# Layer 1's heads: the wait for recurrent states, eight places for them, and three row blocks of the first head loaded early

## The chip, the cores and the metric

The kernel runs on one core of one Trainium2 chip. The metric is the device time of one execution in microseconds; lower is better. The profile is that of one execution of the same program. Engine names are those of the profile: PE is the matrix engine (PEld its weight loads), ACT the scalar engine, DVE the vector engine, POOL the GpSimd engine, SP the engine that only issues transfers.

## The reference, cut to what matters

The program is a two-layer streaming encoder step for 512 prompt tokens and 8 running sequences of 16 tokens each (640 tokens, width 2048). Layer 0 is stick-breaking attention; layer 1, which this change is in, is gated linear attention (GLA) with 4 heads, 256 key and 512 value channels each:

```
q_in = q * exp(b)                                     # b: running sum of the log decays
a = einsum('bchd,bshd->bhcs', q_in, k * exp(-b)), kept for s <= c
o = einsum('bhcs,bshe->bche', a, v) + einsum('bchd,bhde->bche', q_in, S)
S = exp(b_last)[..., None] * S + einsum('bshd,bshe->bhde', k * exp(b_last - b), v)
o = o * rsqrt(mean(o * o) + EPS) * g_out
y = (o * silu(r)) @ w_out
```

The prompt starts from a zero state S and goes through it in blocks. Each of the 8 running sequences brings a state of its own (256 x 512 floats a head) that is read from HBM, used, updated and written back. After the heads, y = (4 heads x 512 channels) @ w_out, with the 2048 rows of w_out handled as 16 row blocks of 128 (kt 0 to 15; head h owns kt 4h to 4h+3).

## The kernel before, in words

Every product of two full-precision numbers is done as three products of rounded parts (hi x hi, hi x lo, lo x hi). `halves` makes the parts: ACT casts the high one (L134), DVE subtracts to get the low one (L135).

The order of PE's instructions is the order in which the Python program emits them. The other engines' queues are ordered by the compiler's own timeline, so a load on SP or a cast on ACT can run well ahead of the place where it stands in the text, as soon as its data and its place in memory allow. The program keeps a clock of its own, `pe["now"]`, which adds an estimate for each matmul. Around a main stream of matmuls it runs side lanes: Python generators that `yield step(wait, tp, z, tiled)` and are resumed by `Side.tick`, which the main stream calls every few matmuls, once `wait` on that clock has passed. In `tick`, lanes that are due and not marked `tiled` run first; then follows

```
            tiled = [x for x in due if x in self.lanes and x[1][2]]
            if tiled and pe["now"] >= self.tiled_at + self.every:
```

The list `due` was made at the start of the tick. A lane that has just run in this tick, and now stands at a `tiled` step, is in that list still; it is run a second time at once, and the wait of its new step is not looked at.

The stage of this change is "layer 1's heads". Its main stream is, in this order:

- `others` (L653, in `plain`): the q and k products of heads 1 to 3, 12 of them in 24 items of 48 matmuls of 320 columns. It ends with head 3's k. The h2 operand lies in the 32 large places t0 to t31; the 12 places t20 to t31 are free once the last item but one has ended.
- `share(0)`, then `share(1)` (L699): the output product's rows of head 0 (kt 0 to 3) and of head 1 (kt 4 to 7), 240 matmuls of 512 columns each. `share(g)` may begin when `came["rows"] >= 4 * g + 4` row blocks are split into the places, and 2.0 us of the program's clock after the last of them; until then `side.until` lets only the side lanes run and moves the clock on by 0.2.
- the tail (L368, L2004): rows of heads 2 and 3, residual, norm and stores.

The side lanes are:

- `decays`: decay factors of a head (L1638 on PE, tables of exp and log on ACT), then q and k scaled by them. Head 3's waits for the end of `others`.
- `prompt_lane`: 4 blocks of 128 tokens a head; scores L1566, products L1554, state S; it ends each block with `leave`, which transposes (L1601), multiplies by the gate (DVE L1602) and stores to `og_d[h]` (POOL L78, shown as og<-gate).
- `sample_lane`: the running sequences of a head, in 4 groups of 4 states: read each state with q (L1864, 8 matmul records a group), then update each (PE L1870, DVE L1872), store it, and ask for a new one in its place. There are `S0 = 7` places; an `ask` (POOL, shown as s<-in_state_gla) comes 7.0 us of the program's clock after the store (out_dram<-s) of the state that had the place. Before reading a group the lane does

```
                    while any(x not in states for x in group):
                        yield step(0.3)
                    yield step(max(since, max(states[x][1] for x in group) + 13.0) - pe["now"], tiled=True)
```

where `states[x][1]` is the clock at the ask. The step ahead of this one is never `tiled`.

- `fetches`: reads finished rows of `og_d` back (SP L71, shown as og_in<-og) into the two places of the tag "pl", which hold the outputs of `others` too, and splits them (`ogh`, `ogl`). All of kt 0 to 3 are asked for behind `came["last"]`, which is set in the middle of the last item of `others`, when the last output has its place.

The transfers of POOL (state loads and stores, gates, og<-gate) are issued in one queue, in order.

Of the kernel before, what the change touches and what calls it, by code (L numbers as in the profile page):

```python
# [8 lines left out]
F32 = mybir.dt.float32  # L9
# [6 lines left out]
P = 128  # L16
# [14 lines left out]
ZSCALE = 128 ** -0.5  # L31
TOK = T // P
WR = 2
S0 = 7
GP = 2
NPAIR = HEADS // 2
PLAIN = 2
# [4 lines left out]
def hybrid_step_kernel(ctx: ExitStack, tc: tile.TileContext, A: dict, O: list):  # L42
# [27 lines left out]
    def load(out, in_):  # L70
        nc.sync.dma_start(out=out, in_=in_)  # L71
# [61 lines left out]
    def halves(hi, lo, x, e=None):  # L133
        nc.scalar.copy(hi, x)  # L134
        (e or dve).tensor_tensor(lo, x, hi.bitcast(F32), op=ALU.subtract)  # L135
# [13 lines left out]
    def wraw(src, a, n):  # L149
        r = wp.tile([P, 1024], F32, tag="wr", name="wr", bufs=WR)[:, :a * n]  # L150
        load(r.rearrange("p (a n) -> p a n", a=a), src)
        return r
# [113 lines left out]
    def slot(n, shape=(P, T), dt=F32R, name="h"):  # L266
        return hp.tile(list(shape), dt, tag=f"t{n}", name=name)
# [6 lines left out]
    def step(wait=0.0, tp=0, z=0, tiled=False):  # L274
        return wait, tp, z, tiled

    class Side:
# [10 lines left out]
        def after(self, wait, what):  # L288

            self.due.append((pe["now"] + wait, what))  # L290
            self.due.sort(key=lambda x: x[0])

        def share(self, **bufs):
            self.free = {k: [0.0] * n for k, n in bufs.items()}
# [52 lines left out]
    def drive(*gens):  # L347
        for g in gens:
            for _ in g:
                side.tick()  # L350
# [331 lines left out]

    y_t = {}

    def share(g, og, w, leave=None, at=None, first=None):


        src = w.rearrange("(kt p) n -> p kt n", p=P)

        def raw(c, i):  # L690
            return wraw(src[:, 4 * g + 2 * i:4 * g + 2 * i + 2, 512 * c:512 * c + 512], 2, 512)

        def products(acc, a, i, w):
            wh, wl = w
            for e in range(2):
                kt = 4 * g + 2 * i + e
                h, lo = (x[:, P * a:P * a + P] for x in og[kt])
                for l, r, first, last in ((h, wh, True, False), (h, wl, False, False), (lo, wh, False, True)):
                    mm(acc, l, by(l, r[:, e, :]), start=i == 0 and e == 0 and first, stop=i == 1 and e == 1 and last)  # L699
                yield  # L700

        def add(a, c, pt):
            if g:
                dve.tensor_tensor(y_t[a, c], pt, y_t[a, c], op=ALU.add)  # L704
            else:
                y_t[a, c] = slot(5 * c + a, (P, 512), F32, "y")
                nc.scalar.copy(y_t[a, c], pt)

        leave = leave or add
        raws = list(first or [raw(0, 0), raw(0, 1)])  # L710

        def made():
            return [t.rearrange("p (a n) -> p a n", a=2) for t in split(raws.pop(0))]

        w0, w1 = made(), made()
        for c in range(4):
            ws = [w0, w1]
            if c < 3:
                raws += [raw(c + 1, 0), raw(c + 1, 1)]
            if at:  # L720
                at(c)
            each = (0, 1, 2) if leave is add or c < 3 else (4, 1, 2, 3, 0)
            for a in each:
                acc = bank("mm")
                for i in range(2):
                    yield from products(acc, a, i, ws[i])
                leave(a, c, acc)
                if a == each[0] and c < 3:
                    w0 = made()
            if len(each) == 3:  # L730
                acc = {a: bank("mm") for a in (3, 4)}
                for i in range(2):
                    for a in (3, 4):
                        yield from products(acc[a], a, i, ws[i])
                        if i:
                            leave(a, c, acc[a])
                    if i == 0 and c < 3:
                        w1 = made()
# [491 lines left out]
    with tc.tile_pool(name="o0", bufs=1, reuse_waits="tile") as po, ExitStack() as only_d:  # L1230
# [235 lines left out]
        n = 0  # L1466
# [32 lines left out]
    def w_of(g, c, i):  # L1499

        k0 = 4 * g + 2 * i
        return w_out1.rearrange("(kt p) n -> p kt n", p=P)[:, k0:k0 + 2, 512 * c:512 * c + 512]

    with tc.tile_pool(name="gl", bufs=1, reuse_waits="tile") as gl:
        came = {"plain": False, "last": False, "of": 0, "when": 0.0}

        def keep(dst, hh):
            t = []

            def leave(nt, pt):  # L1510
# [4 lines left out]
                if nt:  # L1515
                    nc.scalar.dma_start(out=dst[:, hh, :], in_=t[0])
                    for h in range(1, GH):
                        if hh and dst is gk_d[h]:
# [3 lines left out]

        others = plain(h2, src, [(n0 + P * hh, keep(dst, hh)) for h in range(1, GH)
                                 for n0, dst in ((256 * h, gq_d[h]), (NK + 256 * h, gk_d[h])) for hh in range(2)],
                       lambda: came.update(plain=True))
        for _ in range(2):
            next(others)

# [24 lines left out]
            for n, (a, b) in enumerate(((0, 0), (0, 1), (1, 0))):  # L1553
                mm(out, l[a], by(l[a], r[b]), start=start and n == 0, stop=stop and n == 2, skip_group_check=True)  # L1554

        masked = [gl.tile([P, P], F32, name=f"aT{n}") for n in range(3)]
        for t in masked:
            nc.gpsimd.memset(t, 0.0)
        turns = {"n": 0}
# [49 lines left out]
        def decays():  # L1609

            def weights(h):
                wa2 = gl.tile([96, 256], F32R, tag="wa2", name="wa2", bufs=2)
                load(wa2.bitcast(F32), wa2_d[:, 256 * h:256 * h + 256])
                yield step(4.0 if h else 8.0)
                return wa2
# [183 lines left out]
        def sample_lane():  # L1799
# [12 lines left out]
            for h in range(GH):  # L1812
# [43 lines left out]
                for n in range(4):  # L1856
                    dt, e = n // 2, n % 2
                    group = [(h, e, dt, m) for m in range(4)]
                    while any(x not in states for x in group):
                        yield step(0.3)  # L1860
                    yield step(max(since, max(states[x][1] for x in group) + 13.0) - pe["now"], tiled=True)
                    for m in range(4):
                        l = qz[e][:, dt, 32 * m:32 * m + 32]
                        mm(o[32 * m:32 * m + 32, :], l, by(l, states[group[m]][0]), start=False, stop=n == 3,  # L1864
                           skip_group_check=True)
                    for m in range(4):
                        yield step(0.3, tp=1)
                        pt = bank("tp")
                        l = kst[e][:, m, :]
                        mm(pt, l, by(l, vst[:, m, :]), start=True, stop=True)  # L1870
                        s0 = states[group[m]][0]
                        dve.scalar_tensor_tensor(s0, s0, es[:, dt, 2 * m + e:2 * m + e + 1], pt,  # L1872
                                                 op0=ALU.mult, op1=ALU.add)
                        side.after(1.0, lambda x=group[m]: leaves(x))
                    if n == 1:
                        yield from stack(1)
                        yield step(1.5)
# [5 lines left out]
                if h + 1 < GH:  # L1883
                    yield step(4.0)
                    here = fetch(h + 1)

        def fetches():

            def free(kt):
                g, s = kt // 4, kt % 4  # L1890
                return came["plain"] and came["shares"] >= min(2, g if s > 1 else g - 1)

            rows = {}

            def ask_rows(kt):
                rows[kt] = gl.tile([P, T], F32, tag="pl", name="og_in", bufs=2)
                load(rows[kt], og_d[kt // 4][:, kt % 4, :])

            for kt in range(10):
                while min(through.values()) <= kt // 4 or not came["last"]:  # L1900
                    yield step(0.5)
                if kt not in rows:
                    yield step(5.0)
                    ask_rows(kt)
                    if kt % 4 < 3 and kt < 9 and came["plain"]:
                        ask_rows(kt + 1)
                    yield step(4.0)
                while not free(kt):
                    yield step(0.3)
                n = 20 + 2 * kt % 12  # L1910
                og1[kt] = slot(n, name="ogh"), slot(n + 1, name="ogl")
                halves(*og1[kt], rows.pop(kt))
                if kt % 4 < 3 and kt < 9 and kt + 1 not in rows:
                    ask_rows(kt + 1)
                came["rows"], came["at"] = kt + 1, pe["now"]
                yield step(0.5)
# [2 lines left out]
        for x in (decays(), prompt_lane(), sample_lane(), fetches()):  # L1919
            side.add(x)  # L1920
        drive(others)
        with tc.tile_pool(name="w4", bufs=1, reuse_waits="tile") as w4:
            ring3["pool"] = w4
            first = [wraw(w_of(0, 0, i), 2, 512) for i in range(2)]
            for g in range(2):
                side.until(lambda: came["rows"] >= 4 * g + 4 and pe["now"] > came["at"] + 2.0)
                drive(share(g, og1, w_out1, first=first))
                came["shares"] = g + 1
                first = [wraw(w_of(g + 1, 0, i), 2, 512) for i in range(2)]
            ring3["pool"] = None  # L1930
            parts = [split(r) for r in first]
            first = [wraw(w_of(3, 0, i), 2, 512) for i in range(2)]
            side.finish()


    share_banks(mm=8)
# [96 lines left out]
```

## Time and profile before

| what | before |
|---|---|
| median of 3 runs | 2536.63 us (2534.40 to 2538.53) |
| the profiled execution's own time | 2535.51 us |
| its span from first to last instruction | 2533.8 us |
| PE busy | 2429.8 us (96% of the span) |
| DVE / ACT / POOL busy | 1581.8 / 995.2 / 163.6 us |
| layer 1's heads, `others` | about 1975 to 2243 us |
| `share(0)`, first to last matmul | 2266.8 to about 2353 us |
| `share(1)`, first to last matmul | about 2354 to 2411 us |

A row of the timeline has start and length in microseconds, engine, line, operation, tiles, count; in brackets stands how long the engine had been idle before it and what ended that. A row of the waits has who waited for whom: microseconds in total, times, longest. A row of a table by stretches has, for each engine, busy time and count, then the granted clock of PE (1.00 is full), the share of the DMA engines and GB/s.

### The profile page before, as it was taken

To read this page: it belongs to the slowest core of one execution; us is meant where nothing else is said; L and a number is where in the kernel's file an instruction comes from. 1 tells how busy PE (TensorE), PEld (TensorE's weight loads), DVE (VectorE), ACT (ScalarE), POOL (GpSimd) and SP (SyncE) were. 2 spreads that over 40 slices of the span, in tenths; PEclk is the share of its full clock that TensorE was granted. 3 is DMA by queue.
4 is the path that set the end of the run, shared out by engine and by line. 5 is a ranking of instruction groups with operands and counts; after the bars stand their busy time and mean duration, and the time that the engine had idled before them with its cause. 6 is when DMAs were issued, how large, how long until landed. Compare 5 with 4: busy or idle time off the path is not lost. (4 is left out here: it accounts for less than half of the span.)

```text
span 2533.8 us, 43960 instructions
## 1 busy us (share of the span) xinstructions
PE 2429.8 (96%) x17561; PEld 2150.1 (85%) x17561; DVE 1581.8 (62%) x2565; ACT 995.2 (39%) x1730; POOL 163.6 (6%) x390
## 2 busy tenths in 40 slices
PE   7899999999999989999999989999999999979998
PEld 5589999999999989888887768999999988857776
DVE  5575555555656655766775678666676565555556
ACT  4342222222223334555442345333333554545223
POOL 0010000000000000000000000000000233342100
PEclk8899999999999999999999999999999999989999
DMA  9966666766654357777864655354434778785634
GB/s 346 327 209 212 223 214 198 241 218 205 219 186 123 113 187 233 260 246 243 267 209 124 214 172 169 96 148 123 125 105 119 212 238 255 217 278 184 228 111 147
DMA packets 469439, 503.13 MB, mean 199 GB/s; under 512 B 42730, under 2 KB 366450, under 8 KB 469106
## 3 DMA queue, kind: packets, MB, share of 16 engines
q1 hardware_dynamic: 446274, 436.60, 54.8%
q0 software_dynamic: 16048, 51.92, 6.1%
q10 hardware_dynamic: 6912, 11.80, 1.3%
q8 instruction: 138, 2.26, 0.4%
q14 instruction: 67, 0.55, 0.1%
HBM read 411.10 MB, written 89.13 MB: 197 GB/s over the span
## 5 line engine op out<-in xcount | busy, mean ns | idle before, releaser
L594 PE MATMUL ps_mm<-sums,wh 128*128 128x320 f32 x2752 | 613.7, 311 | 1.5 <-ACT wh L134 1.5
L594 PE MATMUL ps_mm<-h,wh 128*128 128x320 f32 x2064 | 461.8, 312 | 5.7 <-DVE u L600 4.6
L594 PEld LDWEIGHTS ps_mm<-sums,wh 128*128 128x128 f32 x2752 | 458.3, 188 | 10.4 <-issue 7.4
L594 PE MATMUL ps_mm<-sums,wl 128*128 128x320 f32 x1376 | 425.8, 309 | 0.7 <-DVE wl L135 0.7
L135 DVE TENSOR_TENSOR wl<-wr,wh 128x1024 fp32r<-128x1024 f32 x193 | 236.1, 1224 | 244.0 <-ACT wh L134 243.2
L594 PEld LDWEIGHTS ps_mm<-h,wh 128*128 128x128 f32 x2064 | 343.2, 188 | 21.8 <-issue 13.0
L134 ACT CAST wh<-wb 128x1024 fp32r<-128x1024 f32 x170 | 178.4, 1049 | 426.1 <-PE ps_mm L594 352.8
L134 ACT CAST wh<-wr 128x1024 fp32r<-128x1024 f32 x193 | 202.6, 1050 | 346.6 <-PE ps_mm L594 184.6
L594 PE MATMUL ps_mm<-h,wl 128*128 128x320 f32 x1032 | 319.2, 309 | 0.0
L653 PE MATMUL ps_mm<-h,wh 128*128 128x320 f32 x1152 | 265.2, 318 | 5.3 <-ACT pl L1514 3.1
L594 PEld LDWEIGHTS ps_mm<-sums,wl 128*128 128x128 f32 x1376 | 258.4, 188 | 1.0 <-DVE wl L135 1.0
L135 DVE TENSOR_TENSOR wl<-wb,wh 128x1024 fp32r<-128x1024 f32 x170 | 207.9, 1223 | 60.5 <-ACT wh L134 60.1
L653 PEld LDWEIGHTS ps_mm<-h,wh 128*128 128x128 f32 x1152 | 193.0, 189 | 21.7 <-issue 11.4
L699 PE MATMUL ps_mm<-wh,ogh 128*128 128x512 f32 x450 | 197.4, 439 | 4.2 <-DVE y L704 2.7
L594 PEld LDWEIGHTS ps_mm<-h,wl 128*128 128x128 f32 x1032 | 193.8, 188 | 0.0
L653 PE MATMUL ps_mm<-h,wl 128*128 128x320 f32 x576 | 178.5, 310 | 0.0
L699 PE MATMUL ps_mm<-wh,ogl 128*128 128x512 f32 x450 | 177.9, 395 | 0.3 <-DVE ogl L135 0.3
L699 PE MATMUL ps_mm<-wl,ogh 128*128 128x512 f32 x450 | 177.7, 395 | 0.0
L699 PEld LDWEIGHTS ps_mm<-wh,ogh 128*128 128x128 f32 x450 | 85.6, 190 | 29.6 <-issue 14.4
L653 PEld LDWEIGHTS ps_mm<-h,wl 128*128 128x128 f32 x576 | 108.8, 189 | 0.0
L699 PEld LDWEIGHTS ps_mm<-wh,ogl 128*128 128x128 f32 x450 | 85.0, 189 | 20.3 <-DVE ogl L135 0.7
L518 PE MATMUL ps_mm<-wh,h 128*128 128x512 f32 x252 | 93.4, 432 | 5.9 <-ACT h L134 2.8
(355 smaller groups left out, 3747.0 us busy)
## 6 DMA issues: line engine op xcount, KB each, us to landing
ar<-in_w_ada_dram SPq DMA_DIRECT2D x160, 512.0 KB
wb<-in_sb_w_in_dram SPq DMA_DIRECT2D x82, 512.0 KB
kc<-in_cache_sb_k_dram SPq DMA_DIRECT2D x64, 512.0 KB
vc<-in_cache_sb_v_dram SPq DMA_DIRECT2D x64, 512.0 KB
wr<-in_gla_w_in_dram SPq DMA_DIRECT2D x51, 512.0 KB
wb<-in_gla_w_in_dram SPq DMA_DIRECT2D x45, 512.0 KB
wr<-in_sb_w_in_dram SPq DMA_DIRECT2D x44, 512.0 KB
ar<-in_w_ada_dram SPq DMA_DIRECT2D x64, 256.0 KB
```

Of the source, the lines that this page charges most:

```text
L134: nc.scalar.copy(hi, x)
L135: (e or dve).tensor_tensor(lo, x, hi.bitcast(F32), op=ALU.subtract)
L518: mm(acc[a], l, by(l, r[:, e, :]), start=j == 0 and e == 0 and begun, stop=j == 7 and e == 1 and last)
L594: mm(acc, l[:, k, :], by(l[:, k, :], r), start=start and k == 0 and first, stop=k == 7 and last, skip_group_check=True)
L653: mm(acc[nt], l[:, k, :], by(l[:, k, :], r), start=k0 == 8 and k == 0 and first, stop=k0 == 0 and k == 7 and last)
L699: mm(acc, l, by(l, r[:, e, :]), start=i == 0 and e == 0 and first, stop=i == 1 and e == 1 and last)
```

## The change: what it does

- The wait of a group of states is split into a step that is not `tiled`, `max(since, last ask + 9.0)`, and a `tiled` step of 0.0 behind it, so that the wait is kept.
- `S0` goes from 7 to 8. The memory for it comes from `wa2` (one place instead of two) and from two of the three `masked` tiles, which now lie in the shift and scale tables of layer 1's norm.
- The pool `w4` (a third pair of places for split weights, before opened behind `others`) is opened with the stage. When head 0 is done in both lanes, 8.0 later, kt 0, 1 and 2 of `og_d[0]` are loaded into its two tiles (four loads: kt 2 is cut in two pieces). They are split when the last item but one of `others` has ended. Only kt 3 still goes through "pl", without the extra wait of 5.0.
- `upper()`, called at the end of the last item but one, starts `share(0)`'s generator there: its first two weight loads and the first split are emitted at that place.

```diff
-S0 = 7
+S0 = 8
...
-        w0, w1 = made(), made()
+        w0 = made()
+        if apart:
+            yield
+        w1 = made()
...
-                       lambda: came.update(plain=True))
+                       lambda: upper())
...
-        masked = [gl.tile([P, P], F32, name=f"aT{n}") for n in range(3)]
+        masked = [t[1].rearrange("p k r -> p (k r)")[:, :P] for t in (sh_t, sc_t)] + [gl.tile([P, P], F32, name="aT2")]
...
-                wa2 = gl.tile([96, 256], F32R, tag="wa2", name="wa2", bufs=2)
+                wa2 = gl.tile([96, 256], F32R, tag="wa2", name="wa2")
...
-                    yield step(max(since, max(states[x][1] for x in group) + 13.0) - pe["now"], tiled=True)
+                    yield step(max(since, max(states[x][1] for x in group) + 9.0) - pe["now"])
+                    yield step(0.0, tiled=True)
...
+        begun = []
+
+        def upper():
+            came.update(plain=True)
+            begun.append(share(0, og1, w_out1, first=[wraw(w_of(0, 0, i), 2, 512) for i in range(2)], apart=True))
+            next(begun[0])
...
+            while min(through.values()) < 1:
+                yield step(0.5)
+            yield step(8.0)
+            x = [w4.tile([P, 1024], F32, tag=t, name="og_in") for t in ("wh", "wl")]
+            for n in range(2):
+                load(x[n][:, :T], og_d[0][:, n, :])
+            load(x[0][:, T:], og_d[0][:, 2, :1024 - T])
+            load(x[1][:, T:2 * T - 384], og_d[0][:, 2, 1024 - T:])
+            while not came["plain"]:
+                yield step(0.3)
+            for kt in range(2):
+                halves(*row(kt), x[kt][:, :T])
+                yield step(0.8)
+            to = row(2)
+            halves(*[t[:, :1024 - T] for t in to], x[0][:, T:])
+            halves(*[t[:, 1024 - T:] for t in to], x[1][:, T:2 * T - 384])
+            came["rows"], came["at"] = 3, pe["now"]
...
-            for kt in range(10):
+            for kt in range(3, 10):
                 while min(through.values()) <= kt // 4 or not came["last"]:
-                    yield step(0.5)
+                    yield step(0.3)
                 if kt not in rows:
-                    yield step(5.0)
+                    if kt > 3:
+                        yield step(5.0)
                     ask_rows(kt)
-                    if kt % 4 < 3 and kt < 9 and came["plain"]:
+                    if 3 < kt < 9 and kt % 4 < 3:
                         ask_rows(kt + 1)
                     yield step(4.0)
```

A second `self.due.sort` was added too; it sorts a list that is sorted already.

More of the change, by code (lines that the diff above doesn't have):

```diff
@@ L290, in after @@
             self.due.append((pe["now"] + wait, what))
+            self.due.sort(key=lambda x: x[0])
             self.due.sort(key=lambda x: x[0])
@@ L683, in hybrid_step_kernel, with share @@
     y_t = {}
-    def share(g, og, w, leave=None, at=None, first=None):
+    def share(g, og, w, leave=None, at=None, first=None, apart=False):
         src = w.rearrange("(kt p) n -> p kt n", p=P)
@@ L1502, in w_of @@
         return w_out1.rearrange("(kt p) n -> p kt n", p=P)[:, k0:k0 + 2, 512 * c:512 * c + 512]
-    with tc.tile_pool(name="gl", bufs=1, reuse_waits="tile") as gl:
+    with tc.tile_pool(name="gl", bufs=1, reuse_waits="tile") as gl, \
+            tc.tile_pool(name="w4", bufs=1, reuse_waits="tile") as w4:
         came = {"plain": False, "last": False, "of": 0, "when": 0.0}
@@ L1885, in sample_lane, with row @@
                     here = fetch(h + 1)
+        begun = []
[3 more added lines that the diff above has]
+            next(begun[0])
+        def row(kt):
+            n = 20 + 2 * kt % 12
+            og1[kt] = slot(n, name="ogh"), slot(n + 1, name="ogl")
+            return og1[kt]
         def fetches():
@@ L1890, in free @@
                 g, s = kt // 4, kt % 4
-                return came["plain"] and came["shares"] >= min(2, g if s > 1 else g - 1)
+                return came["shares"] >= min(2, g if s > 1 else g - 1)
+            while min(through.values()) < 1:
[15 more added lines that the diff above has]
+            came["rows"], came["at"] = 3, pe["now"]
             rows = {}
@@ L1909, in fetches @@
                     yield step(0.3)
-                n = 20 + 2 * kt % 12
-                og1[kt] = slot(n, name="ogh"), slot(n + 1, name="ogl")
-                halves(*og1[kt], rows.pop(kt))
+                halves(*row(kt), rows.pop(kt))
                 if kt % 4 < 3 and kt < 9 and kt + 1 not in rows:
@@ L1921, in hybrid_step_kernel @@
         drive(others)
-        with tc.tile_pool(name="w4", bufs=1, reuse_waits="tile") as w4:
+        for g in range(2):
+            side.until(lambda: came["rows"] >= 4 * g + 4 and pe["now"] > came["at"] + 2.0)
             ring3["pool"] = w4
[L1924 to L1933, printed above, removed]
+            drive(share(g, og1, w_out1, first=first) if g else begun[0])
+            came["shares"] = g + 1
+            first = [wraw(w_of(g + 1, 0, i), 2, 512) for i in range(2)]
+        ring3["pool"] = None
+        parts = [split(r) for r in first]
+        first = [wraw(w_of(3, 0, i), 2, 512) for i in range(2)]
+        side.finish()
     share_banks(mm=8)
```

## The prediction, as put on record before the changed kernel ran

> **What bounds the kernel.** I read first the page, then PE's waits over the stage, then PE's timeline at each long wait, then the queues that feed what PE waited for. First the page's busy times and PE's waits from 1966 to 2420 us:
>
> ```profile
> PE 2429.8 (96%) x17561; PEld 2150.1 (85%) x17561; DVE 1581.8 (62%) x2565; ACT 995.2 (39%) x1730; POOL 163.6 (6%) x390
> ...
> PE ps_z L1864 <- DMA s<-in_state_gla_dram: 23.4, 3, 17.4
> ...
> PE ps_mm L368 <- DVE y L704: 1.5, 1, 1.5
> PE ps_mm L699 <- DVE y L704: 1.1, 3, 0.5
> PE ps_mm L699 <- ACT y L707: 0.9, 1, 0.9
> ```
>
> PE is the bound, and nearly all that it loses in this stage is one wait: sample states that are not there when L1864 reads them. The three cases on PE's timeline, with the last matmul of `others` and the first of `share(0)`:
>
> ```profile
> 2081.52 1.04 PE L1864 MATMUL ps_z<-s,qz 128*32 128x512 f32 x2 [0.26 <-DMA s<-in_state_gla_dram]
> ...
> 2170.20 1.92 PE L1864 MATMUL ps_z<-s,qz 128*32 128x512 f32 x2 [5.69 <-DMA s<-in_state_gla_dram]
> ...
> 2242.95 0.31 PE L653 MATMUL ps_mm<-h,wl 128*128 128x320 f32 x1
> 2243.10 0.86 PE L1870 MATMUL ps_tp<-vst,kst 128*128 128x512 f32 x3
> ...
> 2245.82 1.06 PE L1864 MATMUL ps_z<-s,qz 128*32 128x512 f32 x6
> 2264.32 1.92 PE L1864 MATMUL ps_z<-s,qz 128*32 128x512 f32 x2 [17.44 <-DMA s<-in_state_gla_dram]
> 2266.16 0.80 PE L1870 MATMUL ps_tp<-vst,kst 128*128 128x512 f32 x1
> 2266.76 0.63 PE L699 MATMUL ps_mm<-wh,ogh 128*128 128x512 f32 x1
> ```
>
> Each time the first three states of a group are there (x6) and the fourth is not. A wait costs more than its length, since PE comes back at a lower clock (stretches; clock after POOL's column):
>
> ```profile
> 2170.00:2174.00 4.00, 3.80 (x9) 2.14 (x10) 0.65 (x3) 1.20 (x4) 0.91 (x2) 0.50 0.45 143
> 2264.30:2267.00 2.70, 2.68 (x4) 0.93 (x5) 0.00 (x1) 0.69 (x2) 0.75 (x1) 0.50 0.92 324
> 2267.00:2271.00 4.00, 4.00 (x12) 3.11 (x12) 2.15 (x4) 1.69 (x3) 1.69 (x3) 0.59 0.23 87
> ```
>
> Length times missing clock: 4.0 x 0.50 + 2.7 x 0.50 + 4.0 x 0.41 = 5.0 us. So the three waits cost 0.26 + 5.69 + 17.44 + 5.0 = 28.4 us.
>
> The Trainium skill, "TensorE: Matmul & The Clock Gate", section "What's actually happening", states that the clock is halved after an idle window of about 3.4 us and comes back after a busy one as long. By that figure two waits would cost 2 x 3.4 x 0.5 = 3.4 us of clock, an estimate from that page; the sum would then be 26.8. The trace agrees on the half clock (0.50) and has it last longer after the second wait.
>
> **The change part by part.** *The wait that is now kept.* The 13.0 us of before are never waited: the step ahead is not tiled, so the lane runs on in the same tick. Head 0 shows it:
>
> ```profile
> 2033.81 1.07 PE L1864 MATMUL ps_z<-s,qz 128*32 128x512 f32 x8
> 2037.18 0.39 PE L1870 MATMUL ps_tp<-vst,kst 128*128 128x512 f32 x1
> ...
> 2041.89 0.39 PE L1870 MATMUL ps_tp<-vst,kst 128*128 128x512 f32 x1
> 2047.54 1.06 PE L1864 MATMUL ps_z<-s,qz 128*32 128x512 f32 x8
> ```
>
> With 7 places the second group's fourth state takes the place of the first state updated (2037.18). It is asked for 1.0 + 7.0 later, about 2045.2, and a kept wait would put the read at 2058 or later; it comes at 2047.54, just behind the ask. So the read stands wherever the poll falls, and PE runs into any delay of POOL. The largest shows in POOL's queue:
>
> ```profile
> 2251.60 0.76 POOL L78 DMA_DIRECT2D gate<-gr  x1 [1.57 <-issue]
> ...
> 2258.89 0.72 POOL L78 DMA_DIRECT2D og<-gate  x1 [5.99 <-DVE ogl L135]
> 2259.53 1.68 POOL L78 DMA_DIRECT2D s<-in_state_gla_dram  x3
> ```
>
> The updates ahead of that read are those at 2243.10 and one before, so the ask is due by 2251 on PE's time; four state loads stand behind an og<-gate that is held for 5.99 us, the first of them is the missing one, and PE stands.
>
> *Eight places* let all four states of the next group stay in place while one group is worked on. A group's states take the places of the group before the last; the last is asked for about 8 us (with the ticks up to 10) behind the fourth update, and read 9.0 later. From the rows: fourth update at 2041.89 - 2033.81 = 8.1, so reads of a head come at 0, about 9.5 (states long there), 8.1 + 10 + 9 = 27 and about 36.5. Head 0's last read ends with the row of 2081.52, 47.7 after its first; so the lane is a little faster in spite of the wait. What does it wait for now? From the ask, the issue may be held by POOL, and the load takes its time:
>
> ```profile
> POOL gate L78 <- DMA og<-gate: 18.5, 6, 5.0
> ...
> POOL og L78 <- DVE y L1640: 6.1, 1, 6.1
> POOL og L78 <- DVE ogl L135: 6.0, 1, 6.0
> ...
> s<-in_state_gla_dram POOLq DMA_DIRECT2D x64, 256.0 KB, 4.8
> ```
>
> Median 4.8 us to landing and a hold of 18.5 / 6 = 3.1 make 7.9, under 9.0. With a hold as in the case above (5.99) it is 10.8, 1.8 over. Eight groups (two a head) hang on a late ask; if all met such a hold it would be 8 x 1.8 = 14 us, if none 0. I take one hold at a bad place, 2 us: the two rows of 6 us are the only ones of that length, so the typical case is the nearer.
>
> By the Trainium skill, "DMA: Bandwidth & Descriptors", section "Anatomy of one DMA — SWDGE (gpsimd) path", a transfer takes about 2.0 us and its bytes at 436 GB/s, an estimate of 2.6 us for 256 KB. By that the 9.0 us always do and this term is 0; the 4.8 us of the trace speak against the page here.
>
> *Early row blocks.* The gap at 2243 to 2266 has a second cause, right under the first:
>
> ```profile
> 2233.18 0.42 SPq L71 DMA_DIRECT2D og_in<-og  x1
> ...
> 2243.47 0.32 SPq L71 DMA_DIRECT2D og_in<-og  x1
> ...
> 2250.15 0.32 SPq L71 DMA_DIRECT2D og_in<-og  x1
> ...
> 2260.38 0.72 ACT L134 CAST ogh<-og_in 128x640 fp32r<-128x640 f32 x1 [2.75 <-DMA og_in<-og]
> ...
> 2261.14 0.83 DVE L135 TENSOR_TENSOR ogl<-og_in,ogh 128x640 fp32r<-128x640 f32 x1 [0.70 <-ACT ogh L134]
> ```
>
> Each load waits until the row before it is split, since "pl" has two places; kt 3 is ready at 2261.97. With the states alone mended, the gap would still last nearly as long. Now kt 0 to 2 are loaded when head 0 is done, 8.0 behind the last transpose of its sample lane, whose store is this one:
>
> ```profile
> 2105.82 0.73 POOL L78 DMA_DIRECT2D og<-gate  x1 [0.50 <-issue]
> ...
> DMA to landing us min/median/max: 2.7/3.8/5.8
> ```
>
> The second row is that of all such stores: it has landed by 2111.7, and the loads stand near 2113 on SP, so the v and weight loads queued behind them there, each issued well ahead of its use, are not held. Were SP to reach them early, they would be held 5.8 us at most. That is over 100 us before kt 0 is used. They are split during the last item (4 casts of at most 0.72 and 4 subtractions of at most 0.83, 3.3 us on DVE, beside 48 matmuls), and kt 3 can take the load at 2233, ready by 2243. So `share(0)` can begin when `others` ends. Cost 0. A bound: the load of 2250.15 was used before the cast at 2260.38, so a row takes under 10.2 us and 1.6 for its split: 2245, 2 us behind the end of `others`; but kt 3 comes last of the four, so at most 1 us would show. Four early loads instead of three add one issue to SP, about 0.4 us.
>
> *The rest, at 0.* `upper()` emits two loads and a split earlier, but SP issued the weights ahead already, the second of them here:
>
> ```profile
> 2219.36 0.38 SPq L71 DMA_DIRECT2D wr<-in_gla_w_out_dram  x1
> ```
>
> What covers them is the last items of `others`; without that cover the first split (1.06 on ACT and 1.23 on DVE, by the tail's pieces below) would show, 2.3 us. One `wa2` place: a head's decays are done on PE before the next table is asked for, and heads lie far apart; without that cover a table's landing (some 4.8) would show at three heads, 14 us. The `masked` tiles need the same three memsets, ahead of everything here.
>
> *What is late next.* First, all of head 3's decays now run beside `share(0)`, where ACT also empties its two banks; the half that did so before cost the 0.9 us on "ACT y L707". I add 1 (bounds 0 and 3). Second, the chain of waits ends in this stage's tail:
>
> ```profile
> 2361.81 3.02 DMA og<-gate
> ...
> 2390.17 4.10 DMA wr<-in_gla_w_out_dram
> ...
> 2394.37 1.06 ACT wh L134
> 2395.45 1.23 DVE wl L135
> ...
> 2397.42 13.23 PE ps_mm L699 x56
> ```
>
> The sample lane's last store frees a train of SP loads, and PE meets its last weights 35.6 us later with no slack. Both sides move up. Head 3's lane hangs on the end E of `others` as before: its last og<-gate was at E + 118.8, less 17.44 and 3.0 of clock E + 98, and less about 3 for its faster reads E + 95, so its train ends at E + 131. PE came there at E + 154.4; less the same 20.4 and less the waits of 0.9, 1.1 E + 132, and a few us of head 2's lane (seven L1870, one group of L1864, about 3 us) now lie before E: E + 129. So it waits about 2 us (bounds 0 and 7).
>
> **Sum.** -28.4 + 2 + 1 + 2 = -23.4 against the profiled execution's 2535.51: 2512.1. That execution stood 1.1 under the median of 2536.63, so against the median 2513.
>
> **The rivals.**
> 1. *The tail's train decides.* If head 3's reads are no faster and POOL holds its last stores once (6 us), the train ends at E + 140 and PE waits 11 instead of 2: 2522. For it: no slack now. Against: the lane gets shorter on paper.
> 2. *Only the long gap goes.* og<-gate still jams POOL behind each head's last block, and the new reads run into it as at 2170: 5.69 and 2.0 of clock stay, 2513 + 8 = 2521, and a second of that kind makes 2529; between them 2525. For it: POOL's one queue is left as it is. Against: 9 us of grace.
> 3. *Slower.* The kept wait is too short where places come free together: four stores and four loads a burst, in one queue. It decides if each of the eight late groups stands over 28.4 / 8 = 3.6 us, that is, if states land over 12.6 us behind the ask; at 5 us each it is 40 - 28.4 = 12 slower, 2548. The longest hold and landing in the rows (5.99, 4.8) make 10.8.
> 4. *Nothing changes*: another wait, such as kt 3's, fills the gap: about 2535.
>
> **How the numbers follow.** Chances: forecast 0.65, rival 1 0.13, rival 2 0.11, rival 4 0.05, rival 3 0.06. The lower end is the full 28.4 with the small waits of 0.9, 1.1 and 1.5 gone too: 2536.6 - 31.9 = 2505. The upper end takes in rivals 1 and 2: 2528. The forecast's own range is 2505 to 2520. About 0.2% (5 us) is what a measurement can tell from no change; faster by more is 0.65 + 0.13 + 0.11 = 0.89, within it 0.05, slower 0.06.
>
> **What would show it.** Right: no L1864 wait over 2 us on states; `share(0)`'s first matmul within 3 us of the last L653; the clock 1.00 from 2236 to 2275; og_in for kt 0 to 2 near 2115; reads of a head spaced about 9.5, 17.5, 9.5. Wrong: L1864 rows with idle in brackets at the third or fourth read of heads; a long "DVE y L704" wait near the end of `share(1)`, the train; or an L699 row waiting on ogl at the start of `share(0)`.

## The result, and the profile after

| | before | after | ratio (95% interval) |
|---|---|---|---|
| first comparison, us (median, range) | 2535.86 (2533.37 to 2540.05) | 2517.46 (2512.60 to 2522.88) | 0.9927 [0.9912, 0.9943] |
| second comparison, us | 2537.61 (2535.08 to 2543.50) | 2518.70 (2515.59 to 2522.67) | 0.9924 [0.9912, 0.9937] |
| profiled execution, us | 2535.51 | 2512.6 (span 2510.9) | |

The change gains 18.4 us, and 18.9 us the second time. The forecast was 2513, a gain of 23.4. The profiled execution of the changed kernel is the fastest of its six. In the changed kernel lines move by one to six: the read L1864 is L1870, the update L1870 is L1876, L653 is L654, L699 is L700, L368 is L369, L1566 is L1571, L1601 is L1606, L1583 is L1588. First the page's busy times:

```profile
PE 2420.5 (96%) x17561; PEld 2145.2 (85%) x17561; DVE 1580.8 (63%) x2566; ACT 993.2 (40%) x1731; POOL 164.9 (7%) x390
```

PE has the same 17561 instructions and is busy 9.3 us less, 4.1 of it in this stage (the windows below) and 5.1 ahead of it. Then PE's waits from 1966 to 2420 us (what waited, for what; us in total, times, longest):

```profile
PE ps_tp L1571 <- DVE k L1669: 4.5, 2, 3.2
PE ps_mm L700 <- ACT y L708: 3.4, 3, 2.7
PE ps_mm L654 <- ACT pl L1519: 3.1, 2, 2.1
PE ps_mm L700 <- DVE y L705: 1.7, 4, 0.7
PE ps_mm L369 <- DVE y L705: 1.5, 1, 1.5
PE ps_tp L1876 <- DVE s L1878: 1.3, 1, 1.3
PE ps_tp L1876 <- DVE gate L1607: 0.9, 1, 0.9
PE ps_mm L654 <- DVE out L601: 0.7, 1, 0.7
PE ps_tp L1876 <- DVE S L1762: 0.4, 1, 0.4
```

The row that was 23.4 us, L1864 on states, is gone altogether. What is left is 16 waits of 0.3 to 3.2 us on ACT and DVE. Where `others` gives way to `share(0)`, PE's timeline now reads:

```profile
2232.19 0.31 PE L654 MATMUL ps_mm<-h,wl 128*128 128x320 f32 x1
2232.34 0.60 PE L1606 MATMUL ps_tp<-ident,on 128*128 128x128 f32 x4
2232.87 1.07 PE L1870 MATMUL ps_z<-s,qz 128*32 128x512 f32 x8
...
2235.46 0.50 PE L1876 MATMUL ps_tp<-vst,kst 128*128 128x512 f32 x1 [0.40 <-DVE S L1762]
2236.86 0.49 PE L1876 MATMUL ps_tp<-vst,kst 128*128 128x512 f32 x1 [0.90 <-DVE gate L1607]
2238.65 0.50 PE L1876 MATMUL ps_tp<-vst,kst 128*128 128x512 f32 x1 [1.29 <-DVE s L1878]
2238.98 0.39 PE L700 MATMUL ps_mm<-wh,ogh 128*128 128x512 f32 x1
```

All eight read records stand in one row, so all four states are there, and instead of the 17.44 us gap there are lane matmuls with 2.6 us of waits between them. The clock in the stretch of that gap, and in the two stretches at half clock that are left (PE's busy time first, PEclk behind the last bracket):

```profile
2236.00:2275.00 39.00, 33.37 (x147) 24.96 (x148) 27.20 (x47) 25.98 (x48) 15.66 (x27) 1.00 0.88 281
...
2090.10:2093.50 3.40, 3.40 (x15) 3.40 (x14) 0.67 (x3) 1.17 (x3) 1.32 (x2) 0.50 1.15 309
2165.20:2168.60 3.40, 3.40 (x16) 3.36 (x15) 2.83 (x5) 2.60 (x8) 2.85 (x6) 0.50 0.98 365
```

The clock is 1.00 where it was halved, and 2 x 3.40 x 0.50 = 3.4 us of work are lost elsewhere, one stretch right behind the wait on k of 3.24 us, the other behind one on pl of 2.09. By windows of 1 us the kernel before loses about 5.2 us of work in this way in the whole stage, so this profile gains 1.8.

**Where the time went.** The stage from its first restart (the row of 0.7 us on `out`) to the first matmul of the tail (that of 1.5 us at L369), by windows of PE alone: before, then after.

```profile
1975.36:2413.01 437.65, 404.97 (x2292) 0.97 0.73 230
```

```profile
1972.46:2390.12 417.66, 400.83 (x2293) 0.99 0.76 241
```

The stage is 20.0 us shorter: 32.7 - 16.8 = 15.9 us less idle and 404.97 - 400.83 = 4.1 us less busy with the same matmuls. Of the 4.1 the clock explains 1.8. By lines all of it lies in the reads, busy 21.9 us before and 17.0 after, while the rest rises by 0.8: each late state had left its two matmul records to run by themselves (1.04, 1.92 and 1.92 us in the rows of before). The spans differ by 22.9; the other 2.9 us lie ahead of the stage (it starts at 1972.46 instead of 1975.36), in code that the change does not touch.

### The profile page after: what moved, and what is told of

It is laid out like the page before. It is cut to its first block, busy times and chain, and to the rows that moved or that the text cites. A ratio compares the mean times of both kernels' runs of the same rounds, so it can differ in the third digit from the quotient of the medians.

```text
span 2510.9 us, 43987 instructions
## 1 busy us (share of the span) xinstructions
PE 2420.5 (96%) x17561; PEld 2145.2 (85%) x17561; DVE 1580.8 (63%) x2566; ACT 993.2 (40%) x1731; POOL 164.9 (7%) x390
## 5 line engine op out<-in xcount | busy, mean ns | idle before, releaser
L135 DVE TENSOR_TENSOR wl<-wr,wh 128x1024 fp32r<-128x1024 f32 x193 | 236.0, 1224 | 237.2 <-ACT wh L134 236.6
L654 PE MATMUL ps_mm<-h,wh 128*128 128x320 f32 x1152 | 266.1, 318 | 5.4 <-ACT pl L1519 3.1
L135 DVE TENSOR_TENSOR wl<-wb,wh 128x1024 fp32r<-128x1024 f32 x170 | 207.9, 1223 | 61.2 <-ACT wh L134 60.5
L654 PEld LDWEIGHTS ps_mm<-h,wh 128*128 128x128 f32 x1152 | 194.3, 190 | 20.1 <-issue 8.9
L700 PE MATMUL ps_mm<-wh,ogh 128*128 128x512 f32 x450 | 196.8, 437 | 7.5 <-ACT y L708 3.7
L654 PE MATMUL ps_mm<-h,wl 128*128 128x320 f32 x576 | 179.2, 311 | 0.0
L700 PE MATMUL ps_mm<-wh,ogl 128*128 128x512 f32 x450 | 177.3, 394 | 0.3 <-DVE ogl L135 0.3
L700 PE MATMUL ps_mm<-wl,ogh 128*128 128x512 f32 x450 | 176.9, 393 | 0.0
L700 PEld LDWEIGHTS ps_mm<-wh,ogh 128*128 128x128 f32 x450 | 84.9, 189 | 34.3 <-issue 15.0
L654 PEld LDWEIGHTS ps_mm<-h,wl 128*128 128x128 f32 x576 | 109.4, 190 | 0.0
L700 PEld LDWEIGHTS ps_mm<-wh,ogl 128*128 128x128 f32 x450 | 84.6, 188 | 20.2 <-DVE ogl L135 0.7
```

What stands on the lines that cost most here:

```text
L654: mm(acc[nt], l[:, k, :], by(l[:, k, :], r), start=k0 == 8 and k == 0 and first, stop=k0 == 0 and k == 7 and last)
```

## The experiments

They ran in three groups, each on one chip beside the kernel before, whose medians were 2537.63, 2537.61 and 2537.87 us. Ratios are to that kernel, and runs of different groups are compared by them.

**One part alone: the states** (`e1_states_alone`). The kernel before with

```diff
-S0 = 7
+S0 = 8
-                    yield step(max(since, max(states[x][1] for x in group) + 13.0) - pe["now"], tiled=True)
+                    yield step(max(since, max(states[x][1] for x in group) + 9.0) - pe["now"])
+                    yield step(0.0, tiled=True)
```

and the memory moves that make room for it. Nothing of the rows or of `upper()`.

> The kernel before with eight places and the kept wait of 9.0 only; rows, upper() and the pool w4 as before. Theory (two causes lie on top of each other where others ends: a state that is not there, and the row chain of kt 0 to 3): the states' waits go (L1864 waits under 2 us in all, before 23.4), but share(0) still cannot begin before kt 3 is split, some 15 to 19 us behind the last L653; gain 6 to 11 us, 2525 to 2530. Rival A (the state was the only cause): share(0) begins within 5 us of the last L653 and the time is that of the whole change, about 2517.

Measured: 2532.80 us against 2537.63, ratio 0.9983 [0.9973, 0.9992]. No read (L1865 here) waits for a state. PE's timeline at the start of `share(0)`, and SP's queue for the same time:

```profile
2247.07 0.39 PE L699 MATMUL ps_mm<-wh,ogh 128*128 128x512 f32 x1
...
2263.53 0.79 PE L699 MATMUL ps_mm<-wh,ogh 128*128 128x512 f32 x1 [14.05 <-ACT ogh L134]
```

```profile
2241.49 0.32 SPq L71 DMA_DIRECT2D og_in<-og  x1
...
2247.31 2.21 SPq L71 DMA_DIRECT2D og_in<-og  x2
```

PE stands 14.05 us at the same place, now for a row block. The wait was handed over, 17.44 to 14.05: there is a second cause under the first. It is not simply the chain of loads that the prediction had named, as the queues of ACT, DVE and POOL show:

```profile
2260.38 0.69 ACT L1583 ACTIVATE on<-ps_z,on_r 128x512 f32<-128x512 f32 x1 [10.48 <-POOL on_r L234]
...
2262.77 0.71 ACT L134 CAST ogh<-og_in 128x640 fp32r<-128x640 f32 x1
```

```profile
2247.93 0.14 DVE L232 TENSOR_SCALAR on_ms<-oss 128x1 f32<-128x1 f32 x1
```

```profile
2259.71 0.63 POOL L234 TENSOR_TENSOR on_r<-on_ms,mhalf 128x1 f32<-128x1 f32 x1
```

The cast of the row stands in ACT's queue behind the sample lane's scaling, and that stood 10.48 us for L234, a power on POOL. The input of the power was there at 2247.93; POOL's queue of transfers came to it at 2259.71. The last two loads were issued by 2249.52, and the cast did not wait for them, so how long the loads alone would have held PE is not shown. In the changed kernel the last of the four rows is cast at 2233.92, ahead of the scaling that ACT stands for there (2248.95), and so is free of either cause. The gain of 4.8 us is less than the 6 to 11 that I expected; PE's waits on pl and on k have grown as well (6.3 and 3.4 us, before 3.1 and 1.6).

**The other part alone: the rows** (`e2_rows_alone`). The changed kernel with `S0 = 7` and the single tiled step of 13.0.

> The changed kernel with seven places and the old single step of 13.0 whose wait is not looked at; rows and upper() as changed. Theory: the rows are split in time, but the sample states are still read right behind the ask; the waits of L1870 (the read's new line) on states stay at 15 to 25 us in all; gain 0 to 8 us, 2528 to 2536. Rival B (the row chain was the cause, and held POOL's store and so the state): states' waits fall under 8 us and the time is within 5 us of the whole change, 2517 to 2522.

Measured: 2546.92 us, ratio 1.0038 [1.0023, 1.0052]: slower than before. PE's waits on states and on the start of `share(0)`:

```profile
2171.53 1.92 PE L1869 MATMUL ps_z<-s,qz 128*32 128x512 f32 x2 [6.40 <-DMA s<-in_state_gla_dram]
2249.73 0.50 PE L700 MATMUL ps_mm<-wl,ogh 128*128 128x512 f32 x1 [3.25 <-DVE wl L135]
2263.69 1.91 PE L1869 MATMUL ps_z<-s,qz 128*32 128x512 f32 x2 [7.27 <-DMA s<-in_state_gla_dram]
...
2358.23 1.91 PE L1869 MATMUL ps_z<-s,qz 128*32 128x512 f32 x2 [6.05 <-DMA s<-in_state_gla_dram]
```

The long gap is split: the early rows let PE go on into `share(0)`, and it meets missing states 7.27 us there and 6.05 us in `share(1)`, where the kernel before had none. States cost 19.7 us where they cost 23.4, and the wait on a split weight of 3.25 us is new. The stage (1972.73 to 2419.22) is 8.8 us longer than before: 2.9 us more idle and 5.9 more busy, since PE does about 22 us of its work at half clock, before about 10. The mechanism that was expected (15 to 25 us of state waits) is there; the gain of 0 to 8 us is not. With the first run: the states alone give 4.8 us by the medians, the rows alone cost 9.3, both together give 18. The gap had two causes in parallel, and only taking away both opens it.

**Eight places, wait not kept** (`e3_wait_skipped`). The changed kernel with one step:

```diff
-                    yield step(max(since, max(states[x][1] for x in group) + 9.0) - pe["now"])
-                    yield step(0.0, tiled=True)
+                    yield step(max(since, max(states[x][1] for x in group) + 9.0) - pe["now"], tiled=True)
```

> The changed kernel with eight places, but the wait in one tiled step as before, so that it is not looked at. Theory: the third and fourth reads of a head fall right behind the last ask again, and L1870 waits on states by the 4 to 10 us that a load takes in several of the eight cases: 10 to 25 us in all with the clock; 2525 to 2540. Rival C (eight places are enough, the wait does nothing): no state waits over 3 us, 2515 to 2520.

Measured: 2534.48 us, ratio 0.9993 [0.9983, 1.0003]. Nearly all of the gain is gone, but not to the wait that I had expected. PE's waits from 1966 to 2420:

```profile
PE ps_tp L1606 <- ACT on L1588: 18.3, 4, 7.7
PE ps_mm L700 <- DVE y L705: 4.9, 4, 2.8
```

There is no row on states (the read is L1869 here): eight places alone were enough against those waits. PE stands at the transposes of the normed output instead. The longest but one of these four waits, on PE, on POOL, and the norm on DVE:

```profile
2089.77 1.12 PE L1606 MATMUL ps_tp<-ident,on 128*128 128x128 f32 x4 [6.38 <-ACT on L1588]
```

```profile
2081.35 3.13 POOL L78 DMA_DIRECT2D vst<-gv  x6 [1.89 <-issue]
...
2085.61 0.56 POOL L234 TENSOR_TENSOR on_r<-on_ms,mhalf 128x1 f32<-128x1 f32 x1
```

```profile
2076.81 0.15 DVE L232 TENSOR_SCALAR on_ms<-oss 128x1 f32<-128x1 f32 x1
```

The mean square is there at 2076.81, and the 0.56 us power on it begins at 2085.61: 8.8 us in POOL's queue of transfers. And ACT, which needs it, then runs the next head's decays first, and comes to the scaling at 2089.04. The single step also brings both lanes to their norms together: ACT squares the two outputs at 2071.83 and 2073.00 here, at 2062.38 and 2073.40 in the changed kernel. That suggested what to try.

**Only the turn later** (`e5_turn_later`). The same kernel, and in the sample lane

```diff
                 on = scaled_by(*on)
-                yield step(7.0, tp=1)
+                yield step(12.0, tp=1)
                 leave(h, NP, on, g)
```

> The eight-place kernel with the single tiled step of 9.0 (2534.5 us, no wait on states, but 18.3 us in which the PE stood at L1606 for the scaled output of L1588), and the budget ahead of the sample lane's own turn raised from 7.0 to 12.0, so that the four transposes of L1606 stand some 5 us later in the PE's order. Theory A (POOL's queue): the power of L234, which the scaling on ACT needs, is held 8.8 and 10.6 us in POOL's queue behind transfers that are themselves held, and the turn only stands too early on the PE for that; with 5 us more in between, the waits of L1606 on L1588 fall from 18.3 to below 8 us, the half-clock stretches with them, and the time comes to 2518 to 2528. Theory B (ACT): it is the next head's decays, which run on ACT between the power and the scaling, that are in the way, and a turn moved past them only meets the next piece of lane work that is late; the PE's waits in the stage stay above 15 us in sum and the time at 2530 to 2540.

Measured: 2519.83 us against 2537.61, ratio 0.9924 [0.9912, 0.9937], the interval of the changed kernel beside it.

```profile
PE ps_tp L1719 <- ACT on L1588: 6.1, 1, 6.1
PE ps_tp L1606 <- ACT on L1588: 5.6, 3, 3.3
```

The time and L1606 are as theory A has it: L1606 falls from 18.3 to 5.6, with 6.1 at L1719 instead, and 15 us come back with a wait that is still skipped. PE's waits in the stage still sum to 20.6 us (31.3 with the turn of 7.0), above the 15 of theory B, which the time speaks against. The power is as late as before in the sample lane of heads 0 to 2 (8.7, 5.3 and 11.6 us behind its norm, 8.8, 6.8 and 10.5 with the turn of 7.0), so it is only the later turn on PE that helps. The edit moves the turn past POOL's queue and past ACT's decays alike, and does not tell which of the two counts for more. So what the skipped wait costs, 16 us, is a turn that stands too early in PE's order, and not the states. That the kept wait sets this right by putting the lane's end later is read from the timelines, and was not tested by itself. The transfers of states are in time either way, though in the kernel with the skipped wait only just (head 0's last group is read at 2067.49, 3.4 us behind the issue of its last load).

**Seven places, wait kept** (`e4_seven_places`). The changed kernel with `S0 = 7`.

> The changed kernel with the kept wait of 9.0, but seven places. Theory: the fourth state of a group is asked for behind the first update, so a head's reads stand 18 us apart and its sample lane takes some 55 us for the four instead of 36; no waits on states, but head 3's last store comes some 18 us later against share(1), and the train of loads behind it holds PE at the end of share(1): 8 to 20 us; 2524 to 2537. Rival D (the kept wait does it, the places do nothing): 2515 to 2520.

Measured: 2540.09 us, ratio 1.0012 [1.0003, 1.0020]. Here the lane crawls: reads of head 0 at 2042.4, 2066.3, 2089.6 and 2112.9, some 23 us apart (9.0, 19.2 and 9.7 in the changed kernel; 18 were expected here). `share(1)` ended at 2392.3, only 3.6 us later than in the changed kernel (2388.7), and then PE ran out of work, waiting for head 3's lane. Its waits from 2392 on, and POOL's last store of the gated output:

```profile
PE ps_z L1870 <- DMA s<-in_state_gla_dram: 6.9, 2, 4.7
PE ps_tp L1848 <- DVE kc L1843: 2.9, 1, 2.9
```

```profile
2420.89 0.72 POOL L78 DMA_DIRECT2D og<-gate  x1 [1.92 <-DVE gate L1607]
```

That store comes 73 us later than the changed kernel's (2347.77). I had expected 18 us, no wait on states, and 2524 to 2537: the direction was right, the size was not. So the eighth place is what makes the kept wait affordable.

**The changed kernel again, and two mends of what is left.** `e8_changed_again` is the changed kernel. `e6_pool_relieved` moves seven transfers a head from POOL to SP:

```diff
-                    move(sp_o[0, 0, h].rearrange("(d p) v -> p d v", p=P), S)
+                    store(sp_o[0, 0, h].rearrange("(d p) v -> p d v", p=P), S)
...
-                        move(vst[r0:r0 + NT].bitcast(F32), rows)
+                        load(vst[r0:r0 + NT].bitcast(F32), rows)
```

`e7_ready_later` gives DVE more time before a head's first product:

```diff
-                yield step(3.0 if h else 6.0)
+                yield step(6.0 if h < 3 else 3.0)
                 ready[h] = q, k, e1, el, ed, es
```

> The changed kernel itself, once more, beside the other three. Its first six executions ran from 2512.6 to 2522.9 us, the kernel before from 2533.4 to 2540.1: both theories on the size expect a median of 2515 to 2520 here; a profile with the same waits (L1571 on k, L700 on y, no wait on states) would say that they belong to the kernel, other places or sizes would say that they move from execution to execution.

> The changed kernel with seven of POOL's transfers per head moved to SP's queue: the six small loads of the samples' values and the store of the prompt's last state S. Theory A (POOL's queue holds the power of L234 back in the changed kernel too: 6.4, 5.1 and 3.8 us between on_ms and L234 in the sample lane of heads 0 to 2, and the last of these delays the y copies of share(0) on ACT, for which the PE waits 2.68 us): these three delays fall below 2 us, the wait of L700 on the y copies from 3.4 to below 1.5, and the time comes to 2508 to 2514, 3 to 6 us below the changed kernel beside it. Theory B: what holds POOL is the transfers of states and gates themselves, the delays stay, and the time is within 3 us of the changed kernel. Theory C: the loads and the store delay SP's loads of weights by their waits, a new wait on the weights' split appears, and the time is 2520 or more.

> The changed kernel with the budget between a head's decays and its being ready raised from 3.0 to 6.0 for heads 1 and 2 (head 3 keeps 3.0). Theory A: the waits of L1571 on k (3.24 us at head 1's start, 1.26 at head 2's) are the PE reaching the head's first product some 3 us before DVE has scaled k; with 3 us more they go, and the half-clock stretch of 3.4 us behind the first with them: some 4.5 + 1.7 = 6 us less wait, of which the lane's own delay of 3 us per head gives nothing back while the products cover it: 2510 to 2514, 3 to 6 us below the changed kernel. Theory B: the lane is what sets the end (share(1) waits for head 3's outputs), and a lane 6 us later costs as much at the end as the waits gave: within 2 us of the changed kernel, with the waits of L700 in share(1) grown by 3 us or more.

Measured: 2518.70 (the changed kernel), 2516.66, ratio 0.9915 [0.9902, 0.9927] (relieved), 2517.68, ratio 0.9911 [0.9896, 0.9925] (later). None differs from the changed kernel by what can be told. Its second profile has the same waits in the same places with other sizes:

```profile
PE ps_mm L654 <- ACT pl L1519: 6.1, 2, 3.2
PE ps_tp L1571 <- DVE k L1669: 2.6, 1, 2.6
PE ps_mm L700 <- ACT y L708: 1.9, 2, 1.4
```

So these rows belong to the kernel, and single sizes vary by 1.5 to 3 us from execution to execution. With POOL relieved, the power in the sample lane of heads 0 to 2 comes 3.6, 3.5 and 2.5 us behind its norm (6.4, 5.1 and 3.8 in the first profile of the changed kernel, 5.7, 5.8 and 2.0 in the second), which is less for heads 0 and 1 but not under 2 as expected, and worth nothing that shows. With the later budget the waits on k go, and others grow:

```profile
PE ps_mm L700 <- ACT y L708: 7.7, 2, 6.5
PE ps_mm L654 <- ACT pl L1519: 7.6, 5, 2.7
```

Neither theory on that run was right: the waits do move, as B has it, but to the copies of `share(0)` and the evictions of pl, and `share(1)` waits no more than before (1.6 us on y).

**Is it ACT's standing for the power?** `f1_scaled_later` is the changed kernel with

```diff
                 on = normed(o)
+                yield step(6.0)
                 on = scaled_by(*on)
-                yield step(7.0, tp=1)
+                yield step(3.0, tp=1)
```

`f2_scaled_and_ready` adds the budget of 6.0 to it, `f3_and_pool_relieved` also the seven transfers on SP. `f4_before_scaled_later` is the kernel before with these lines alone.

> The changed kernel, with the sample lane's scaling of its output (L1588, ACT) taken 6.0 us after the norm instead of right behind it, and the budget to the turn cut from 7.0 to 3.0 (9.0 in all): ACT no longer stands in its own order before POOL's power L234, which comes 3.8 to 6.4 us late. Theory A (one cause): this standing of ACT (5.8 us at 2153.2 and 4.5 us at 2244.4 in the changed kernel) is what makes the evictions of pl and the y copies late, for which the PE waits 3.1 and 3.4 us there; these two rows fall to below 2 us in sum, clock loss with them, and the time comes to 2509 to 2514, 4 to 9 us under the changed kernel (2518). Theory B (no cause): the evictions are late for the table loads and decays of the next head, and the waits only move to another of them; within 2 us of the changed kernel.

> The same, with the budget ahead of a head's being ready raised from 3.0 to 6.0 for heads 1 and 2 as well. By theory A the waits on k (3 us in the changed kernel, 0.4 with the raised budget alone) go and the y copies no longer take their place, since ACT is not held: 2506 to 2512, at least 2 us under the run with the scaling alone. By theory B the raised budget again only moves the waits: within 2 us of the run with the scaling alone.

> Both of these, and the samples' small loads and the store of S on SP's queue. If POOL's delay matters only through ACT's standing, this brings nothing more: within 2 us of the run before it. If late gates and states behind POOL's queue still cost at the end (og_in of the last rows, 1.5 to 2 us of waits on y in share(1)), 2 to 4 us less.

> The kernel before, with the scaling taken later alone, nothing of the change. Theory A expects little, because there the state waits (23.4 us) and the chain of rows set the end whatever ACT does: 0 to 4 us under the kernel before, 2533 to 2537. Were the standing of ACT what the change really mended, this alone would give most of the 18 us: 2518 to 2525.

Measured, against 2537.87: 2520.06, ratio 0.9924 [0.9909, 0.9939]; 2511.92, ratio 0.9900 [0.9883, 0.9917]; 2523.02, ratio 0.9931 [0.9918, 0.9945]; and 2539.60, ratio 1.0008 [0.9995, 1.0020]. The first did not do what it was meant to. ACT's waits for the power in the changed kernel, and in that one:

```profile
ACT on L1588 <- POOL on_r L234: 24.2, 11, 5.8
```

```profile
ACT on L1591 <- POOL on_r L1587: 21.7, 12, 6.3
```

The power still came 5.6, 4.2 and 6.0 us behind its norm in the sample lane, about as late as the scaling now stood. So theory A was not put to the test by it. The second has the best median of all kernels here, and 8 us under the first, as theory A had it; but its interval touches that of the changed kernel (0.9924 [0.9912, 0.9937]), the rows do not say where a gain would come from (ACT stands 31.6 us for the power, and PE waits 8.1 us on pl and 5.9 on y), and the third, one edit further, is 11 us above it instead of within 2. I do not call it faster. The fourth shows that this edit gives nothing in the kernel before. It is a weak test, since ACT still stands 13.1 us for the power there (16.8 without the edit); but in the changed kernel ACT stands longer, 24.2 us, and so this standing is not what the change mended.

## Why the prediction was right, point by point

- **State waits, -23.4 and 5.0 of clock.** The waits went to 0, as forecast. The clock term did not come: the half clock behind the state waits went, but 3.4 us are lost at half clock in other places, behind waits on k and pl that the sum did not price, so 1.8 came back. In the second profile about 6.3 us are lost (behind pl twice and once just ahead of `share(0)`), and nothing came back.
- **States landing over 9.0 us, +2.** Mis-sized: 0. A group's last load in POOL's queue and its read on PE in the changed kernel:

```profile
2141.57 0.58 POOL L78 DMA_DIRECT2D s<-in_state_gla_dram  x1 [0.29 <-issue]
```

```profile
2151.24 0.64 PE L1870 MATMUL ps_z<-s,qz 128*32 128x512 f32 x4
```

  That is 9.7 us, against a median landing of 4.9 (4.8 before). The hold of 6 us that the term stood for did not fall on any late ask. By the Trainium skill, "DMA: Bandwidth & Descriptors", section "Anatomy of one DMA — SWDGE (gpsimd) path", the term would be 0 too, at an estimated 2.6 us a load; the term came out as by that page, while the measured 4.9 speaks against its figure.
- **The kept wait.** The reading of `tick` was right, and the spacing of head 0's reads too (9.0, 19.2, 9.7; forecast 9.5, 17.5, 9.5). What failed is the step that gave the wait its worth: "PE runs into any delay of POOL". With eight places and the wait skipped, no read waits. The runs with the skipped wait show in its place that PE meets the transposes of the normed output too early (18.3 us at L1606), and that a later turn is worth as much as the kept wait (ratio 0.9993 without either, 0.9924 with either). That this part of the change paid is luck as far as the prediction goes.
- **Early rows, cost 0.** Right: SP issued three of the loads in one row,

```profile
2103.55 1.33 SPq L71 DMA_DIRECT2D og_in<-og  x3
```

  10 us sooner than the forecast 2113 to 2115 (the fourth stands at 2069.84), and no L700 waits for a row. "With the states alone mended, the gap would still last nearly as long" came true in the first experiment (14.05 of 17.44), but not by the chain of loads alone that the prediction gave for it: there ACT stood 10.48 us for the power on POOL, which the prediction had not seen. But `share(0)` begins 2238.98 - 2232.50 = 6.5 us behind the last L654, not within 3: the lane matmuls that stand there wait 2.6 us on DVE, a term that the sum lacked.
- **Head 3's decays beside `share(0)`, +1 (0 to 3).** PE's wait on ACT's y is 3.4 us where it was 0.9: +2.5 in the first profile, 1.9 and so +1.0 in the second. Inside the bounds.
- **The train at the tail, +2 (0 to 7).** It is met and costs 0.6 (1.7 on y in `share(1)` instead of 1.1). The chain that ended last:

```profile
2347.77 5.98 DMA og<-gate
...
2355.19 5.47 DMA og_in<-og
...
2372.56 1.23 DVE wl L135
...
2374.54 13.22 PE ps_mm L700 x56
```

  The size was near, the working was not: with E = 2232.5 the store stands at E + 115 and PE's last meeting at E + 142, not at E + 95 and E + 129. I had head 2's lane end before E; its last read came 10.0 us behind E (2242.5). Lane and PE moved together, so the error cancelled.
- **Waits that were not in the sum.** k: 4.5 us instead of 1.6, +2.9 (+1.0 in the second profile). pl: 3.1 and 3.1 (6.1 in the second profile).
- **The account.** Idle: -23.4 on states, +2.6 (L1876), +2.5 (y), +2.9 (k), +0.6 (train), and -1.0 for four waits of 0.2 to 0.4 that are gone: -15.8, against 15.9 by the windows. Busy: -4.1. Together -20.0 for the profiled stage; the medians give -18.4, and the second profile of the changed kernel fits that better, since its stage took 420.2 us (1974.94 to 2395.17). From the forecast to the profile: -23.4, less 2 (landing), 1.4 (train) and 1.0 (small waits), and 1.5 (y), 2.9 (k), 2.6 (L1876) and 0.9 (5.0 of clock against 4.1 of busy time) on top, make -19.9. So the total came near, 4.5 us under the median, because terms too high stood against terms missing, all of them small beside the 23.4 us of state waits, which was right.

Of the rivals none came. Rival 2 ("only the long gap goes", 2521 to 2529) is the nearest in time, and is excluded because no read L1870 waits for a state.

## What to carry to other kernels

A gap can have two causes that end within 3 us of each other; the second is read from the queues that run beside the first (here SP's row loads, and ACT's casts of them), and mending one alone may even cost time. A lane's wait also sets a place in the order of the engine that it feeds: before putting a gain down to the data that it waited for, run the kernel with the data safe and the wait skipped. A tiny operation on a queue of transfers (a power of 0.56 us on POOL) was late by 4 to 12 us in these runs, and everything in order behind its reader is late with it.

## What the runs showed of the hardware that I had not expected

- The half clock comes in steps. In the changed kernel each stretch at half clock lasted 3.4 us (from 2090.1 and from 2165.2), in the kernel before 6.8 and 20.5, two and six times that, in the run with the states alone 3.4, 6.8 and 17.1. A wait of 2.09 us (at 2164.63) was enough, while one of 2.68 us (at 2254.93) cost none. The Trainium skill, "TensorE: Matmul & The Clock Gate", section "What's actually happening", has the window at 3413 ns and free-running; the steps agree with it, and so does it that a wait's place matters beside its length. That the clock falls only after a whole idle window of about 3.4 us, as the same section has it, does not fit: the wait of 2.09 us was the longest near that stretch.
- POOL's transfers can stand for about 6 us while what the trace names as the end of the hold is not their data: og<-gate 5.99 us in the kernel before (`DVE ogl L135`; the gate itself was written by 2248.5, the store came at 2258.89), 5.96 in the changed one at 2156.03 (`DVE s L1878`; written by 2148.9). What holds them was not tried.
- The same program differs by 10 us between executions (2512.6 to 2522.9); the kernel before differs by 6.7 us in the same comparison and by 8.4 to 13.9 in the larger sets beside the experiments.
